# Loading the first operands of an attention into the room of finished state-space scans, and projecting its values first

## The chip, the cores and the metric

The kernel runs on one core of one Trainium2 chip. The metric is the device time of one execution in microseconds (us), lower is better; three runs of the kernel before are known, and their median stands for it.

## The reference, cut to what matters

The program computes two layers of a hybrid trunk on 640 tokens (512 latents, 128 of context) of 1024 channels, in float32. In each layer the normalised stream is projected once, and four mixers of 256 channels work on the columns; then come one output projection and a gated feed-forward part.

```
h = rmsnorm(x) * (1 + scale1) + shift1
fa, fb, fc, fd = split(h @ w_in)
oa = rwkv_mixer(fa)        # two scans
ob = retention_mixer(fb)   # two scans in chunks
oc = ssd_mixer(fc)         # state-space, two scans in chunks
od = diff_mixer(fd)        # differential attention
x = x + gate1 * (concat(oa, ob, oc, od) @ w_out)
x = x + gate2 * conv_ffn(rmsnorm(x) * (1 + scale2) + shift2)

def diff_attention(q, k, v, lam):     # per block of 128 queries and head
    s = einsum(q, k) * scale          # two maps m
    pr = softmax(s)
    return (pr[0] - lam * pr[1]) @ v
```

## The kernel before

Every product with weights is made of three passes (high times high, high times low, low times high) of float32r parts. Weights come by DMA on SP's queue through four raw buffers, ScalarE (ACT) casts the high part (line 184) and VectorE (DVE) subtracts the low part (line 185). Matmuls are recorded at line 84. A scheduler of the framework fixes the order of the instructions on each engine from the program order, priorities and its own model of times; on the chip each engine then takes its instructions in that order, and DMA issues stand in the same order on SP and ACT.

In each layer the last projections are a generator, `rest`: six tiles for the retention (`ret_proj`), then `diff_proj`, which makes the queries and keys of the attention in two tiles each (`dq`, `dk`, tile t = 0 and 1, rotated by `rope_tile` on ACT, DVE and GpSimd (POOL), split into two parts and stored to DRAM) and at its end the values `dv` (a product over all tokens by `tok_product`, stored to DRAM). Beside it run generators for the state-space scans (`ssds`), the retention (`ret`) and the modulation of later stages (`mod`). A loop takes steps from them in rounds: one step of `ssds` and of `ret`, half a step of `rest`, three quarters of one of `mod`. When `rest` has ended, `diff_open` closes the pools of the stream h (`hp`) and of the projections (`sp`), opens the pool `ds0` there and issues the twelve loads of the attention's first tile (`diff_load`, line 1189: `qs` and `ks`, six DMAs each; the values and the cached values on ACT's queue). The loads of the second tile (`ds1`) follow when the pools of retention and state-space scans are closed, and so do those of x (line 1645) and of the mixers' outputs (`out_load`: `olo` on ACT's queue, line 453, cast to `ohi` on ACT at line 199, low part on DVE at line 200).

Pools are stacks from the left and the right end of the on-chip memory. A tile that lies where an older tile lay waits for the last use of that tile.

The attention works in 20 units (t, head, tile of queries): products S on TensorE (PE), maximum on DVE (line 1216), exponential on ACT (line 1218), sum of both maps on DVE (line 1224), transposes on PE (line 1237), copies on ACT (lines 1239 and 1240), product with the values. What of the output projection doesn't need the attention (`po`, rows 2, 3, 4, 5, 0, 1 of `ohi`) runs beside it; rows 6 and 7 follow. Then `gw`, a pool of 12 raw buffers opened at the left where the attention's pools lay, takes weights of the modulation (`GF`), whose products run while the next norm is computed.

Of the kernel before, what the change touches and what calls it, by code (L numbers as in the profile page):

```python
# [23 lines left out]
# token columns: latents 0..511, a zero column, context 513..640, a zero column  # L24
# [4 lines left out]
WR = 7  # L29
PO1 = ()  # L30
DP = 9
RS = (0.5, 0.0, 0.75, 1, 1, 1, 0.5)
DU = 100
# [9 lines left out]
# columns of the per-layer parameter block  # L43
# [10 lines left out]
# columns of the constant block  # L54
# [17 lines left out]
def tile_trunk(ctx: ExitStack, tc: tile.TileContext, xT, cT, wmod, win, wv1, wv2, wout, wup, wdn, wlora, gup, pp, srw,  # L72
# [13 lines left out]
    class Pool:  # L86
        """A tile pool that can be closed out of turn; `bufs` per tag."""
# [14 lines left out]
    class Banks:  # L102
        """A half of PSUM: two pairs of banks (for the dense products) or four single banks."""
# [26 lines left out]
    def XMT(name):  # L130
        """a bank beside the dense products"""
        return sbank.tile(name)

# [23 lines left out]
    # silu(c) = u * (1 + tanh(u)), u = c / 2  # L157
# [30 lines left out]
    def w_pair(src, name):  # L188
        """the two halves (four blocks of the contraction each) of one column tile"""
        return [w_split(src[i], 512, f"{name}_{i}") for i in range(2)]  # L190
# [18 lines left out]
    def modulation(l, qs, bank=SMT, burst=False, pool=None):  # L209
        """in steps: one for each tile of weights, or (burst) for four of them"""  # L210
# [23 lines left out]
    def modulation_blocks(blocks, pool, n):  # L234
        """whole blocks, n tiles of weights loaded ahead"""
# [35 lines left out]
    def modulation_behind(l, qs, bank, pool, after):  # L271
        """loads, products and sums a step apart, each behind what runs beside it"""
# [42 lines left out]
    def spread(r, n, name, d, bank=SMT):  # L315
        """r [128 tokens, 5 * n]: rows of channels; n = 1 for all 128 channels, 2 for two heads of 64."""
# [12 lines left out]
    def x_stats(x, xp, name):  # L329
        """1/rms of x per token, spread over the partitions."""  # L330
# [21 lines left out]
    def norm(l, which, x, xp, name, before=None):  # L352
        """the stream h = rmsnorm(x) * g * (1 + scale) + shift, in two parts, zero columns between the streams"""
# [33 lines left out]
    def cm_product(parts, h, name, M=128):  # L387
        """[M channels, 2 halves of the tokens with one column of overlap on each side]"""
# [12 lines left out]
    def tok_product(l, src, n, h, name, dest):  # L401
        """token rows of h @ W: dest [128 tokens, 5, n]"""
# [19 lines left out]
    def conv(ps, out, wl, wc, wr, bias=None, M=128):  # L422
        """centred taps along the tokens, from PSUM"""
        act(v2(out), ps[:M, :, 1:322], AF.Identity, bias=0.0 if bias is None else bias, scale=wc)  # L424
        vstt(v2(out), ps[:M, :, 0:321], wl, v2(out), MULT, ADD)  # L425
        vstt(v2(out), ps[:M, :, 2:323], wr, v2(out), MULT, ADD)  # L426
# [7 lines left out]
    def head_stats(sqs, n, name, floor=None, scale=1.0 / 64, eps=EPS, bank=SMT, tg=""):  # L434
        """sqs: channel tiles [128, T] of squares -> per token and head, 1/sqrt, [128 tokens, 5 * n * len(sqs)]"""
# [8 lines left out]
    # mixer inputs and outputs wait in DRAM for their turn  # L444
# [18 lines left out]
    # ================= RWKV-7 =================  # L463
# [7 lines left out]
    def rw_proj(l, h, key, dv, out):  # L471
        """one projected tile, tokens shifted"""
# [11 lines left out]
    def rw_prep(l, t, f, dv, rw):  # L484
        """half normalised keys, and the values with tokens on partitions"""
# [10 lines left out]
    def rw_values(l, t, f, rw):  # L496
        """values with tokens on partitions: even chunks of 64 in the upper half, odd ones in the lower"""
# [18 lines left out]
    def rw_pre(l, t, d, f, wa, rw, dv, S, need):  # L516
        """up to the scores inside chunks and the right-hand sides"""
# [20 lines left out]
        # log decays, summed inside chunks of 64 with a leading (trailing) zero  # L538
# [40 lines left out]
        # scores inside chunks of 64, transposed: rows (b | k) of token j, columns (a | r) of token i  # L579
# [5 lines left out]
        for g, ms in enumerate(GRP):  # L585
# [12 lines left out]
            # the strict blocks of 32 on the diagonal  # L598
# [12 lines left out]
        def rhs():  # L611
# [4 lines left out]
            for g, ms in enumerate(GRP):  # L616
# [7 lines left out]
                # right-hand sides [a | A_ak v], tokens on partitions, two chunks a pack  # L624
# [15 lines left out]
    def rw_sub(l, t, d, rw, dv, S):  # L640
        """inverses of the 16-blocks of I - A, transposed, by substitution"""
# [19 lines left out]
        # combined to blocks of 32: X1 O X2 beside the diagonal (X2 O X1 backwards)  # L661
# [21 lines left out]
        # and to blocks of 64: what lies beside the diagonal of the inverses is X1 O X2 again  # L683
# [6 lines left out]
        for e in range(2):  # L690
            # empty in this direction
# [24 lines left out]
    def rw_solve(l, t, d, f, rw, dv, y, S):  # L716
        """solve, the chunk maps, the states from chunk to chunk, the outputs"""
# [47 lines left out]
        # states from chunk to chunk; MI = [state (key, value) ; identity]  # L765
# [37 lines left out]
    def rw_end(l, t, f, rw, dv, y):  # L803
# [5 lines left out]
        # group norm over each head  # L809
# [19 lines left out]
    # ================= projections that wait =================  # L829
    def rope_tile(ps, out, tab, sp, nm):  # L830
        """rotary pairs lie 16 partitions apart in every 32; context columns turn by 0"""
# [8 lines left out]
    def silu2(ps, o):  # L840
        """2 * silu, from PSUM"""
# [43 lines left out]
    def diff_proj(l, h, sp):  # L885
        tab = sp.tile([128, 2, 660], tag="tab", name=f"dtab{l}")
        nc.scalar.dma_start(tab[:, :, 0:T], rope[1])
        # queries and keys in two exact parts, the cache behind the keys of the tokens
        for t in range(2):
# [4 lines left out]
            for nm, src, dst in (("ck", ck[:, 0:128], [d_[:, T:T + 128] for d_ in kd]), ("dq", None, qd),  # L894
# [8 lines left out]
                for d_, part in zip(dst, (hi, lo)):  # L903
                    nc.scalar.dma_start(d_, part.bitcast(F32))
                yield
            scr[f"dq{t}{l}"], scr[f"dk{t}{l}"] = qd, kd
        tv = sp.tile([128, 5, 264], tag="tab", name=f"dv{l}")
        tok_product(l, wv2, 256, h, "dv", tv[:, :, 0:256])
        store(f"dv{l}", tv[:, :, 0:256])
# [991 lines left out]
```

## Time and profile before

| | |
|---|---|
| median of three runs | 2267.35 us |
| lowest and highest run | 2264.86 and 2267.46 us |
| span of the profiled execution, first to last instruction | 2266.5 us |
| the profiled execution's own time | not shown apart from its span; the median lies 0.85 us above the span |
| PE busy | 2136.9 us, 94% of the span |
| mean granted clock of PE | 0.963 of full speed |
| DMA | 232.26 MB, 102 GB/s over the span |

A timeline row gives start, duration, engine, line, operation, output and inputs, count and, in brackets, the idle time of the engine before it with what ended it. SPq and ACTq are DMA issues of these engines. A row of a windows answer gives, for one stretch, its length, the busy time of PE, PEld (weight loads), DVE, ACT and POOL with their instruction counts, the granted clock, the share of the 16 DMA engines that was busy, and GB/s.

### The profile page before, as it was taken

To read this page: it belongs to the slowest core of one execution; us is meant where nothing else is said; L and a number is where in the kernel's file an instruction comes from. 1 tells how busy PE (TensorE), PEld (TensorE's weight loads), DVE (VectorE), ACT (ScalarE), POOL (GpSimd) and SP (SyncE) were. 2 spreads that over 40 slices of the span, in tenths; PEclk is the share of its full clock that TensorE was granted. 3 is DMA by queue.
4 is the path that set the end of the run, shared out by engine and by line. 5 is a ranking of instruction groups with operands and counts; after the bars stand their busy time and mean duration, and the time that the engine had idled before them with its cause. 6 is when DMAs were issued, how large, how long until landed. Compare 5 with 4: busy or idle time off the path is not lost. (4 is left out here: it accounts for less than half of the span.)

```text
span 2266.5 us, 41011 instructions
## 1 busy us (share of the span) xinstructions
PE 2136.9 (94%) x16265; PEld 1936.7 (85%) x16265; DVE 1307.2 (58%) x2951; ACT 816.4 (36%) x1603; POOL 275.2 (12%) x468
## 2 busy tenths in 40 slices
PE   6999999979999999999989999999799999999997
PEld 3887887767878899999988888777678899999997
DVE  3687776547564435545457777755475654454553
ACT  4343432226343313323344334332363432232332
POOL 3111122210020000000031111222001100000002
PEclk9999999988989999999999999999799999999998
DMA  6212126575233332222332211365832222222221
GB/s 241 77 55 67 49 80 226 181 213 137 68 94 121 123 87 71 71 79 75 92 89 60 72 51 56 98 221 176 235 102 73 75 75 71 75 73 77 73 72 67
DMA packets 130943, 232.26 MB, mean 102 GB/s; under 512 B 14784, under 2 KB 34752, under 8 KB 130752
## 3 DMA queue, kind: packets, MB, share of 16 engines
q1 hardware_dynamic: 98304, 176.47, 26.4%
q10 hardware_dynamic: 32448, 53.17, 7.2%
q8 instruction: 129, 2.11, 0.4%
q14 instruction: 62, 0.51, 0.1%
HBM read 199.16 MB, written 30.42 MB: 101 GB/s over the span
## 5 line engine op out<-in xcount | busy, mean ns | idle before, releaser
L84 PE MATMUL pu<-hhi_n,wh_up 128*128 128x324 f32 x1408 | 326.9, 314 | 0.6 <-DVE gv L426 0.6
L84 PE MATMUL pu<-hlo_n,wh_up 128*128 128x324 f32 x1408 | 325.9, 313 | 0.5 <-POOL hlo_n L381 0.4
L84 PE MATMUL pu<-hhi_n,wl_up 128*128 128x324 f32 x1408 | 324.5, 312 | 0.0
L185 DVE TENSOR_TENSOR wl_up<-wr_up,wh_up 128x512 fp32r<-128x512 f32 x176 | 123.2, 706 | 236.2 <-ACT wh_up L184 232.5
L84 PEld LDWEIGHTS pu<-hhi_n,wh_up 128*128 128x128 f32 x1408 | 238.1, 190 | 16.1 <-issue 10.0
L84 PEld LDWEIGHTS pu<-hlo_n,wh_up 128*128 128x128 f32 x1408 | 239.5, 190 | 1.9 <-issue 0.8
L84 PEld LDWEIGHTS pu<-hhi_n,wl_up 128*128 128x128 f32 x1408 | 239.3, 190 | 0.0
L184 ACT CAST wh_up<-wr_up 128x512 fp32r<-128x512 f32 x176 | 108.3, 617 | 291.4 <-issue 136.5
L84 PE MATMUL pd<-gh,wh_dn 128*128 128x322 f32 x704 | 162.5, 312 | 0.0
L84 PE MATMUL pd<-gh,wl_dn 128*128 128x322 f32 x704 | 162.4, 312 | 0.0
L84 PE MATMUL pd<-gl,wh_dn 128*128 128x322 f32 x704 | 162.3, 312 | 0.0
L184 ACT CAST wh_dn<-wr_dn 128x512 fp32r<-128x512 f32 x96 | 56.0, 584 | 207.4 <-PE pd L84 148.2
L185 DVE TENSOR_TENSOR wl_dn<-wr_dn,wh_dn 128x512 fp32r<-128x512 f32 x96 | 61.9, 646 | 106.7 <-ACT wh_dn L184 105.9
L84 PEld LDWEIGHTS pd<-gh,wh_dn 128*128 128x128 f32 x704 | 119.6, 190 | 0.8 <-ACT wh_dn L184 0.8
L84 PEld LDWEIGHTS pd<-gl,wh_dn 128*128 128x128 f32 x704 | 119.3, 190 | 0.5
L84 PEld LDWEIGHTS pd<-gh,wl_dn 128*128 128x128 f32 x704 | 119.2, 190 | 0.0
L432 DVE SCALAR_TENSOR_TENSOR x<-pd,mod,x 128x322 f32<-128x322 f32 x144 | 54.5, 434 | 92.4 <-PE pd L84 92.4
L425 DVE SCALAR_TENSOR_TENSOR gv<-pu,pp,gv 128x642 f32<-128x642 f32 x88 | 78.0, 887 | 41.2 <-ACT gv L424 34.8
L84 PE MATMUL po<-ohi,wh_out 128*128 128x320 f32 (+1 forms) x256 | 79.1, 333 | 14.8 <-ACT ohi L199 14.4
L424 ACT ACTIVATE gv<-pu,pp 128x642 f32<-128x642 f32 x88 | 77.8, 884 | 39.0 <-PE pu L84 39.0
L84 PE MATMUL mps<-wr_mod,sc 128*32 128x512 f32 x384 | 77.3, 672 | 2.9 <-DMA wr_mod<-in_wmod 2.9
L426 DVE SCALAR_TENSOR_TENSOR gv<-pu,pp,gv 128x642 f32<-128x642 f32 x88 | 78.0, 886 | 3.1
(742 smaller groups left out, 4521.9 us busy)
## 6 DMA issues: line engine op xcount, KB each, us to landing
wr_mod<-in_wmod SPq DMA_DIRECT2D x192, 256.0 KB, 4.1
wr_up<-in_wup SPq DMA_DIRECT2D x176, 256.0 KB, 2.6
wr_dn<-in_wdn SPq DMA_DIRECT2D x64, 256.0 KB, 2.7
wr_dn<-in_wdn SPq DMA_DIRECT2D x32, 192.0 KB, 2.4
olo<-scr_o ACTq DMA_DIRECT2D x16, 321.0 KB, 4.6
wr_out<-in_wout SPq DMA_DIRECT2D x16, 256.0 KB, 2.6
wr_out<-in_wout SPq DMA_DIRECT2D x32, 128.0 KB, 2.1
x_in<-in_xT SPq DMA_DIRECT2D x8, 321.0 KB, 5.9
```

The source lines that it names most:

```text
L84: last_pe = nc.tensor.matmul(*a, **k).ins
L184: nc.scalar.copy(hi[:, :n], raw[:, :n])
L185: vtt(lo[:, :n], raw[:, :n], hi[:, :n].bitcast(F32), SUB)
L424: act(v2(out), ps[:M, :, 1:322], AF.Identity, bias=0.0 if bias is None else bias, scale=wc)
L425: vstt(v2(out), ps[:M, :, 0:321], wl, v2(out), MULT, ADD)
L426: vstt(v2(out), ps[:M, :, 2:323], wr, v2(out), MULT, ADD)
L432: vstt(xs, halves[j][:, o:o + n], g[:, s:s + 1], xs, MULT, ADD)
```

## The change

The values are projected first in `diff_proj`, before queries and keys. The retention's pool `mr` moves from the right end to the left one, with six raw weight buffers instead of seven (`WR`). When the state-space scans end, `diff_early` closes their pool `mp`, opens the pools of x and of the norm (`xp`, `xq`) and `ds0` at the right end in its place, and issues the first tile's loads there, provided that the first key tile is projected. `diff_open` then opens only the pool of the attention's work tiles, after the loop. `ds0` stays open until the output projection is done. The rate `RS[3]` and the count `DU`, which would start the attention inside the loop after 100 rounds, go; the loop never reached them. All other lines of the diff remove comments.

```
-WR = 7
+WR = 6
     def diff_proj(l, h, sp):
+        tv = sp.tile([128, 5, 264], tag="tab", name=f"dv{l}")
+        tok_product(l, wv2, 256, h, "dv", tv[:, :, 0:256])
+        store(f"dv{l}", tv[:, :, 0:256])
+        nc.scalar.dma_start(o_v[l], tv[:, 4, 0:256])
+        yield
         tab = sp.tile([128, 2, 660], tag="tab", name=f"dtab{l}")
...
+                if nm == "dk":
+                    scr[f"dq{t}{l}"], scr[f"dk{t}{l}"] = qd, kd
                 yield
-            scr[f"dq{t}{l}"], scr[f"dk{t}{l}"] = qd, kd
-        tv = sp.tile([128, 5, 264], tag="tab", name=f"dv{l}")
-        tok_product(l, wv2, 256, h, "dv", tv[:, :, 0:256])
-        store(f"dv{l}", tv[:, :, 0:256])
-        nc.scalar.dma_start(o_v[l], tv[:, 4, 0:256])
...
         mr = Pool(f"rr{l}", {"tokv": 1, "cs": 1, "ld": 3, "kt": 1, "vw": 2, "st": 1, "pt": 2, "qd": 2, "yy": 1, "tmp": 1,
-                             "wraw": WR}, "right")
+                             "wraw": WR})
...
+        def diff_early():
+            mp.close()
+            xps.append(Pool(f"x{l + 1}", {"x": 1}, "right"))
+            xps.append(Pool(f"xq{l + 1}", {"xs": 1, "xq": 3}, "right"))
+            ds0 = Pool(f"ds0{l}", {"v": 1, "qs": 1, "ks": 1}, "right")
+            while f"dk0{l}" not in scr:
+                pump(rest, 1)
+            ld.append(diff_load(l, 0, ds0, nc.sync))
+            xps.append(ds0)
+
         def diff_open():
             sp.close()
             hp.close()
-            ds0 = Pool(f"ds0{l}", {"v": 1, "qs": 1, "ks": 1})
-            ld.append(diff_load(l, 0, ds0, nc.sync))
             dp = Pool(f"dif{l}", {"P": 6, "at": 3, "yy": 2, "sums": 2, "eps": 2})
-            dpools.extend((dp, ds0))
+            dpools.append(dp)
...
                 if n_ in going and step(n_, g_, rate):
                     going.discard(n_)
-            if not dif and step("rest", rest, RS[6]):
-                dif = diff_open()
-                pump(dif, 1)
+                    if n_ == "ssd":
+                        diff_early()
+            step("rest", rest, RS[6])
         pump(mod)
-        if dif is None:
-            pump(rest)
-            dif = diff_open()
-            pump(dif, 1)
+        pump(rest)
         mr.close()
-        mp.close()
-        xp = Pool(f"x{l + 1}", {"x": 1}, "right")
+        dif = diff_open()
+        pump(dif, 1)
+        xp, xq, ds0 = xps
         x = xp.tile([128, KD, T], tag="x", name=f"x_{l}")
-        xq = Pool(f"xq{l + 1}", {"xs": 1, "xq": 3}, "right")
...
         pump(out_part((6, 7)))
         op.close()
+        ds0.close()
```

## Rows read from the trace of the kernel before

**Rows 1.** The page's line of the granted PE clock, 40 slices of 56.7 us

```profile
PEclk9999999988989999999999999999799999999998
```

**Rows 2.** Windows around the attention's start, first layer, then second

```profile
470.00:491.80 21.80, 21.39 (x177) 17.83 (x178) 10.04 (x22) 5.47 (x12) 1.61 (x4) 1.00 0.78 253
491.80:502.10 10.30, 5.93 (x56) 5.25 (x52) 2.89 (x9) 1.97 (x5) 2.07 (x5) 0.71 0.96 268
502.10:510.20 8.10, 1.63 (x7) 1.44 (x7) 0.19 (x2) 0.73 (x1) 1.55 (x1) 0.50 0.89 230
510.20:523.30 13.10, 11.52 (x40) 9.40 (x41) 10.58 (x17) 8.13 (x18) 0.00 (x0) 0.50 0.84 208
523.30:600.00 76.70, 70.14 (x494) 60.42 (x492) 51.12 (x120) 48.17 (x136) 3.95 (x2) 1.00 0.33 93
600.00:635.00 35.00, 34.22 (x230) 33.94 (x231) 22.27 (x52) 11.22 (x22) 7.47 (x11) 1.00 0.30 87
...
1619.00:1626.40 7.40, 1.59 (x6) 1.40 (x6) 0.00 (x0) 0.73 (x1) 1.03 (x1) 0.50 0.92 232
1626.40:1642.60 16.20, 13.25 (x46) 10.57 (x47) 11.66 (x20) 9.22 (x20) 0.00 (x0) 0.50 0.82 203
```

**Rows 3.** Timeline of PE in the first layer

```profile
499.92 1.30 PE L323 MATMUL R_ret<-cs,rsq 128*128 128x128 f32 x5 [2.91 <-DVE rsq L318]
502.09 1.62 PE L84 MATMUL S<-ks,qs 96*128 96x320 f32 x6 [0.87 <-DVE ry L926]
510.19 0.63 PE L84 MATMUL po<-ohi,wh_out 128*128 128x322 f32 x1 [6.47 <-ACT ohi L199]
```

**Rows 4.** Timeline of PE in the second layer

```profile
1618.97 1.62 PE L84 MATMUL S<-ks,qs 96*128 96x320 f32 x6 [1.45 <-DMA ks<-scr_dk0h]
1626.43 0.63 PE L84 MATMUL po<-ohi,wh_out 128*128 128x322 f32 x1 [5.84 <-ACT ohi L199]
```

**Rows 5.** Timeline of SP's DMA issues in the first layer

```profile
475.69 8.91 SPq L1645 DMA_DIRECT2D x<-in_xT  x8
...
491.84 0.38 SPq L1189 DMA_DIRECT2D qs<-scr_dq0h  x1
...
513.20 0.30 SPq L1189 DMA_DIRECT2D ks<-scr_dk0h  x1
...
548.41 5.19 SPq L177 DMA_DIRECT2D wr_mod<-in_wmod  x3
...
568.58 0.91 SPq L177 DMA_DIRECT2D wr_mod<-in_wmod  x2
```

**Rows 6.** Timeline of ACT and its DMA issues in the first layer

```profile
469.98 0.35 ACTq L450 DMA_DIRECT2D scr_o<-sy  x1
...
505.51 2.37 ACTq L453 DMA_DIRECT2D olo<-scr_o  x3
509.41 0.73 ACT L199 CAST ohi<-olo 128x642 fp32r<-128x642 f32 x1 [14.12 <-DMA olo<-scr_o]
```

**Rows 7.** Timeline of DVE in the first layer, at the attention's start

```profile
510.17 0.83 DVE L200 TENSOR_TENSOR olo<-olo,ohi 128x642 fp32r<-128x642 f32 x1 [7.91 <-ACT ohi L199]
510.91 1.55 DVE L1216 TENSOR_REDUCE mx<-S 128x1 f32<-128x640 f32 x2
```

**Rows 8.** The values' product: matmuls, min/median/max ns, first and last start

```profile
L84 PE MATMUL dv<-wh_dv,hhi_n x40: 278/283/388, 470.5 to 491.1; 128*128 128x256 f32 x40
```

**Rows 9.** Timelines of DVE and POOL during the last key tile's rotation, first layer

```profile
475.11 2.00 DVE L837 TENSOR_TENSOR rsdk<-rsdk,dtab 128x642 f32<-128x642 f32 x1
...
477.46 0.83 DVE L838 TENSOR_TENSOR st_dk<-rfdk,rsdk 128x642 f32<-128x642 f32 x1
474.89 1.54 POOL L836 TENSOR_TENSOR rfdk<-rfdk,dtab 128x642 f32<-128x642 f32 x1 [8.53 <-issue]
```

**Rows 10.** PE's idle time before modulation products: 330 to 500, 1450 to 1620 us

```profile
DMA wr_mod<-in_wmod: 5.3, 4
...
DMA wr_mod<-in_wmod: 0.7, 2
```

More of the change, by code (lines that the diff above doesn't have):

```diff
@@ L28 @@
 TAIL = (0, 0, 1, 1)
-WR = 7
+WR = 6
 PO1 = ()
 DP = 9
-RS = (0.5, 0.0, 0.75, 1, 1, 1, 0.5)
-DU = 100
+RS = (0.5, 0.0, 0.75, None, 1, 1, 0.5)
 HP = {"ssd": 300, "mod": 300}
@@ L1549, in tile_trunk @@
         ld, ys, sums, sp2 = [], {}, {}, [0, None]
-        dif, dpools = None, []
+        dpools, xps = [], []
         def bank_s(n_):
@@ L1567, in diff_open @@
             yield from diff(l, units, dp, dv, ld, ys, bank_s, sums, lambda n_: bank_s(n_)[:, 0])
-        ret, going, rounds = ret_all(), {"ssd", "ret"}, 0
+        ret, going = ret_all(), {"ssd", "ret"}
         while going:
             step("mod", mod, RS[2])
-            if dif and rounds >= DU:
-                step("dif", dif, RS[3])
-            if dif:
-                rounds += 1
             for n_, g_, rate in (("ssd", ssds, RS[4]), ("ret", ret, RS[5])):
```

## The prediction

> **What bounds the kernel now.** I read the page first for PE. It is busy over nine tenths of the span, so only stretches in which it stands still or runs at half clock can give time back. The line of the clock dips in few slices [rows 1]; the slices that begin at 453 and 1587 us lead to the starts of the attention, and there I cut windows [rows 2]. The reader is to see three stretches in each layer. While the last projections run, PE is full at full clock (21.39 of 21.80 us). From 491.8 to 502.1 us only the end of the retention is left, a chain over all engines, and the clock falls from full to its lower level, 0.50. From 502.1 to 523.3 us the clock stays there: PE is busy 1.63 + 11.52 = 13.15 of 21.2 us, which at half clock is 6.6 us of full-speed work, so 14.6 us are lost. The second layer loses 23.6 - (1.59 + 13.25) / 2 = 16.2 us from 1619.0 to 1642.6 us. From then on PE does 70.14 / 76.7 = 0.914 of what it could.
>
> Then I asked the timelines what PE waits for there. The first six products S run when the retention has let go of its PSUM bank in the first layer, and 1.45 us late, for the last `ks` that they need, in the second [rows 3, 4]. So the operands' lateness is itself worth 0 and 1.45 us. The long wait comes after S: 6.47 and 5.84 us for the first `ohi` of the output projection [rows 3, 4]. ACT casts `ohi` when `olo` has landed, at 509.41 us, and DVE's fixed order puts the low part of `olo` (510.17 us) ahead of the first maximum of S (510.91 us), though S was done at 503.71 us [rows 6, 7]. The attention so stands 7.2 us behind a load that it doesn't need. The order was fixed with S expected late: its loads can't be issued before 491.84 us, when the values' product, the last reader of h, has ended [rows 5, 8]. The DMA engines are 0.89 and 0.84 busy from 502.1 to 523.3 us [rows 2], with the rest of the first tile's twelve loads (to 513.20 us), those of the second tile and `olo` together.
>
> **The change part by part.**
>
> The values' product is moved, not changed: 40 groups of three matmuls [rows 8], its eight loads, its copies, its store. PE does it behind the retention's projections instead of behind the last key tile; both times it is filler among full rounds, and the number of steps of `rest` up to its end is 13 as before, so the last projected tile falls into the same round and PE reaches the retention's tail at the same time. Cost: nothing, hidden by PE's own queue; if the order slipped by a round, the tail would shift by at most the projection that is left over, which would cover it. What ends at 491 us is now the second key tile, whose rotation and stores follow beside the retention's tail. Its DVE multiplication took 2.00 us beside POOL's 1.54 us, the addition of the same shape 0.83 us [rows 9]. Lower bound 0 (it fits into the waits of the tail), upper bound all of its DVE time that I can see, 2.00 + 0.83 = 2.8 us per layer. Since the tail's engines mostly wait (DVE 2.89 of 10.30 us) [rows 2], I take 0.5 us per layer. The Trainium skill, SBUF — State Buffer, section "Who interferes with whom", says that a DVE instruction with two on-chip inputs contends with a POOL instruction that reads there; the trace agrees with 2.00 against 0.83 us. By that rule alone, with the tail's own POOL operations caught too, the cost would be some 1.2 us per layer instead of 0.5, and the sum 1.4 us worse.
>
> The first tile's loads can start when the last output of the state-space scans is stored (issue 469.98 us [rows 6]) instead of 491.84 us. On SP they stand among the last modulation weights and before x (eight issues in 8.91 us [rows 5]). Twelve loads of 160 to 193 KB are 2.1 MB, at the 253 GB/s of that stretch 8.4 us: done by about 490 to 495 us even behind the weights, well before 502 us. x slips by as much, to about 495 us; its first reader is the first sum behind the output products, after 510 us, so nothing waits. The values and cached values on ACT's queue also leave the tail.
>
> What this gives: S no longer waits for DMA (1.45 us, second layer), and with S expected at once the order should put its maximum before `olo`. Then from 502.1 us the attention fills PE. I take 55% of PE for the first 6 us (the chain through maximum, exponential and sum starts up; DVE and ACT work 10.58 and 8.13 of 13.1 us once it goes [rows 2]), and 95% from there, when `ohi` has come too. The clock comes back, in the trace, at 523.3 us after PE had been busy without a gap from about 516 us, and at 1642.6 us after gaps until about 1632 us; so I estimate 14 us after the start, at about 516 us. First layer, in full-speed work to 523.3 us: (0.55 * 6 + 0.95 * 8) / 2 + 0.914 * 7.2 = 12.0 against 6.6, a gain of 5.4 us. Second layer, from 1617.6 us: 5.45 + 0.914 * 11 = 15.5 against 7.4, a gain of 8.1 us. Together 13.5 us. From below the gain of this part is 0 (order unchanged, loads hidden) and from above all the loss after S, 14.6 + 16.2 = 31 us; I stand near the middle, because half clock at the restart can't be avoided: it fell in the tail, which stays.
>
> The weights' ring of the modulation shrinks from seven to six. PE waited 5.3 and 0.7 us for such weights in these stretches [rows 10]. Lower bound 0, upper bound those waits again, 6.0 us; the loads come in fours and two buffers still run ahead, so I take 0.5 us in all.
>
> `gw` now lies where the attention's work tiles lay, no longer where `ds0` lay. Its twelve loads were issued from 548.41 to 568.58 us [rows 5], when the first tile's half of the attention was through; now they wait for the last units, about 600 us. They are needed at 635 us, and the DMA engines are 0.30 busy from 600 to 635 us [rows 2]. 3.1 MB at 230 GB/s take 13.7 us. Hidden, unless SP puts them before output weights. Lower bound 0, upper bound 13.7 us less the 10 us or so by which four raw and four split buffers run ahead, 4 us per layer; I take 0.5 us per layer.
>
> `mr` on the other side, `xp` and `xq` opened earlier, `ds0` closed later: no instruction and, by the sizes, nearly the same addresses for `mr`; 0, with 2 us to either side.
>
> Sum: 13.5 - 1.0 - 0.5 - 1.0 = 11 us off the profiled span of 2266.5 us. The median is 0.85 us above that span; the same part lies around both, so I take 11 us off the median: 2256.4 us.
>
> **The rivals.**
>
> A, no change: the loads weren't what held the attention. For it: S waited 0 and 1.45 us for them [rows 3, 4]; if DVE still takes `olo` before the maximum, only 1.45 us and an earlier `olo` (at most the two value loads ahead of it on ACT, about 1.3 us a layer) come off. Against: that order is plainly one made for late loads. Gain 1.5 to 4 us: 2263 to 2266 us.
>
> B, slower: the `gw` loads. SP issues in order; if the first of them waits for the end of the attention's outputs and the output weights of rows 6 and 7 stand behind it, PE, at 34.22 of 35.00 us [rows 2], waits with nothing beside it, and the clock falls. It decides when the twelve loads stand ahead of more output weights than the buffers hold, that is, from a delay of some 10 us. Its price, with the gain lost: 4 us plus a half-clock stretch like that of the attention's start (about 4 us) per layer, 16 us against a gain of 11: 2272 us. Against: DMA is idle there, and output weights were issued early.
>
> C, slower: the ring of six doubles the waits for modulation weights (6 us, in stretches where PE has no gap now), and twelve loads on SP hold the last of them behind them, up to 8.4 us a layer; 2267 - 11 + 6 + 10 = 2272 us. Against: these loads carry a raised priority.
>
> D, more: the second key tile runs into the retention's tail and covers it too. From 491.8 to 502.1 us PE does about 5 of 10.3 us at full-speed count; covering it in both layers gives some 10 us more, 2246 us. Against: the counted rounds are the same.
>
> **How the numbers follow.** Forecast 0.48, A 0.23, B 0.12, C 0.07, D 0.10. The forecast's own range is 2250 to 2262 us, by the bounds above. Its time, 2256.4 us, is the prediction. For eight in ten the range leaves out the outer half of D and of B and C: 2246 to 2272 us. A measurement tells about 0.2%, 4.5 us, from no change: faster means below 2262.8 us, slower above 2271.9 us. Faster: 0.48 and D, 0.58. Same: A less a little that ends slower, and the milder ends of B and C, 0.25. Slower: 0.17.
>
> **What would show it.** `qs` and `ks` of the first tile issued before 485 us and landed before S; on DVE the first `mx` before the first `olo`; PE without the 6.5 us gap before `po`; clock 1.00 some 5 to 10 us sooner after S in both layers; `gw` loads at about 600 us, with PE still full to 635 us. I would be wrong if DVE's order stays, if PE shows new waits for `wr_mod` or `wh_out`, or if the last key tile holds up the retention's tail so that S itself comes later than 502 us.

## The result, and the profile after

| | before | after |
|---|---|---|
| median | 2266.83 us (8 runs, 2257.12 to 2269.36) | 2288.69 us (8 runs, 2275.90 to 2301.41) |
| span of the profiled execution | 2266.5 us | 2274.1 us |
| mean granted clock of PE in it | 0.963 | 0.970 |

The change is slower: ratio 1.0118, 95% interval 1.0093 to 1.0143, that is some 27 us (the ratio isn't the quotient of the two medians, which is 1.0096, or 21.9 us). I had predicted 2256.4 us and a range that ends at 2272. The profiled execution is the shortest of the eight after the change. Its granted clock is 0.970, that of the longest run 0.957, and the times between follow the clock: 0.013 of some 2290 us is 30 us, and the runs lie 25.5 us apart. So this trace shows only 7.6 us of the loss, and what it shows as a wait without a fall of the clock may have one in other runs.

First the page of after: the line of PE's clock, to be held against [rows 1], and the group of the modulation's products, with the same group of before under it.

```profile
PEclk9999999989999999999999999999699899999998
...
L83 PE MATMUL mps<-wr_mod,sc 128*32 128x512 f32 x384 | 92.3, 669 | 0.8 <-DMA wr_mod<-in_wmod 0.8
```

```profile
L84 PE MATMUL mps<-wr_mod,sc 128*32 128x512 f32 x384 | 77.3, 672 | 2.9 <-DMA wr_mod<-in_wmod 2.9
```

The clock is as good as before. The same 384 products, each as long as before, kept PE busy for 77.3 us on the page of before and now for 92.3 us, because fewer of them run side by side.

Then I cut both traces at the same events: the end of the gates' projection, the first S, and the first product of the feed-forward (in the second layer the last output product). Windows of before:

```profile
381.90:502.10 120.20, 110.23 (x781) 82.92 (x779) 61.46 (x140) 31.61 (x67) 25.69 (x23) 0.96 0.66 206
502.10:653.20 151.10, 130.75 (x836) 113.41 (x836) 92.56 (x206) 72.90 (x182) 15.01 (x15) 0.88 0.39 110
1499.80:1619.00 119.20, 109.65 (x781) 82.92 (x779) 62.30 (x138) 31.37 (x67) 26.30 (x24) 0.96 0.66 208
1619.00:1754.30 135.30, 120.14 (x770) 107.45 (x770) 84.23 (x185) 68.82 (x175) 12.61 (x14) 0.90 0.40 109
```

The same windows of after:

```profile
376.80:502.10 125.30, 116.44 (x781) 84.25 (x779) 56.61 (x140) 31.40 (x67) 26.71 (x23) 0.96 0.57 181
502.10:652.00 149.90, 127.02 (x835) 110.45 (x835) 94.19 (x206) 72.52 (x182) 15.03 (x15) 0.92 0.42 127
1496.40:1622.20 125.80, 116.61 (x780) 84.27 (x779) 56.49 (x138) 31.41 (x67) 26.71 (x23) 0.96 0.56 180
1622.20:1760.50 138.30, 120.28 (x770) 108.08 (x770) 85.59 (x186) 68.37 (x175) 13.20 (x14) 0.90 0.41 124
```

The loss of this trace stands ahead of the attention: +5.1 and +6.6 us between the gates' projection and the first S, at the same clock and with the same instructions. PE doesn't wait longer there: its idle time falls by 1.1 and 0.4 us, and its busy time grows by 6.2 and 7.0. The modulation's products in the first of these windows, before and after:

```profile
381.90:502.10 120.20, 23.10 (x144) 0.96 0.66 206
```
```profile
376.80:502.10 125.30, 29.69 (x144) 0.96 0.57 181
```

They grow by 6.6 us, and in the second layer by 7.6 (from 22.25 to 29.83). So what this one trace shows is the ring of six; the runs below show that most of the median's loss is another thing. In the first layer S comes at 502.1 us in both kernels all the same, because the gates' projection ends 5.1 us sooner. From S on the difference is -1.2 and +3.0 us, where I expected -5.4 and -8.1.

The waits have changed too. R_gn, R_ret and R_ssd are five transposes each, which spread the factors of a norm over the channels (of the first mixer, the retention and the state-space scans); rkt transposes the retention's keys. The timeline of PE in before, at four waits of the earlier stretch:

```profile
352.71 0.74 PE L323 MATMUL R_gn<-cs,gsr 128*128 128x128 f32 x5 [1.31 <-DVE gsr L318]
368.62 0.74 PE L917 MATMUL rkt<-cs,ldrk 128*128 128x128 f32 x5 [1.30 <-DMA ldrk<-scr_rk]
432.89 0.77 PE L323 MATMUL R_ret<-cs,rsq 128*128 128x128 f32 x5 [2.14 <-DVE rsq L318]
467.36 0.74 PE L323 MATMUL R_ssd<-cs,ssq 128*128 128x128 f32 x5 [1.36 <-DVE ssq L318]
```

and in after, with the attention's start:

```profile
344.99 0.74 PE L322 MATMUL R_gn<-cs,gsr 128*128 128x128 f32 x5 [2.07 <-DVE gsr L317]
363.17 0.74 PE L918 MATMUL rkt<-cs,ldrk 128*128 128x128 f32 x5 [2.95 <-DMA ldrk<-scr_rk]
436.82 1.23 PE L322 MATMUL R_ret<-cs,rsq 128*128 128x128 f32 x5 [3.36 <-DVE rsq L317]
474.63 1.30 PE L322 MATMUL R_ssd<-cs,ssq 128*128 128x128 f32 x5 [1.29 <-DVE ssq L317]
502.09 1.65 PE L83 MATMUL S<-ks,qs 96*128 96x320 f32 x6 [0.89 <-DVE ry L927]
508.77 1.73 PE L83 MATMUL S<-ks,qs 96*128 96x320 f32 x6 [5.04 <-ACT P L1219]
511.56 0.90 PE L83 MATMUL po<-ohi,wh_out 128*128 128x322 f32 x2 [1.06 <-ACT ohi L198]
```

Three of the four waits have grown, all of them ahead of the key tiles that I had watched. Behind the last two, five products take 1.23 and 1.30 us instead of 0.77 and 0.74: there the clock has fallen (behind R_ret it falls in before too, a little later: 0.50 from 436 to 438 us). At the attention the gap before `po` is down from 6.47 us [rows 3] to 1.06, and a new one of 5.04 us stands before the second S. SP's issues in after:

```profile
480.13 0.47 SPq L1190 DMA_DIRECT2D qs<-scr_dq0h  x1
...
508.49 0.43 SPq L1190 DMA_DIRECT2D ks<-scr_dk0h  x1
...
526.29 4.36 SPq L1648 DMA_DIRECT2D x<-in_xT  x8
...
604.05 7.06 SPq L176 DMA_DIRECT2D wr_mod<-in_wmod  x12
```

The first tile is issued from 480 us on, not from 491.84 [rows 5], but its last load still at 508 us, and x 50 us later than before. DVE and ACT in after:

```profile
503.08 1.56 DVE L1217 TENSOR_REDUCE mx<-S 128x1 f32<-128x640 f32 x2 [0.84 <-PE S L83]
...
511.59 0.83 DVE L199 TENSOR_TENSOR olo<-olo,ohi 128x642 fp32r<-128x642 f32 x1 [0.88 <-ACT ohi L198]
```

```profile
503.75 0.33 ACTq L449 DMA_DIRECT2D scr_o<-ry  x1
504.11 0.59 ACTq L452 DMA_DIRECT2D dv<-scr_dv  x1
504.75 0.68 ACTq L1194 DMA_DIRECT2D dv<-in_cvt  x1
506.95 0.83 ACTq L452 DMA_DIRECT2D olo<-scr_o  x2
507.83 0.79 ACT L1219 ACTIVATE P<-S,mx 128x640 f32<-128x640 f32 x1 [9.88 <-DMA dv<-in_cvt]
```

DVE's order has turned as predicted: the maximum (503.08 us) stands ahead of `olo` (511.59), against [rows 7]. But the exponential that needs this maximum stands on ACT behind four kinds of DMA issues, and starts at 507.83 us. The wait has moved from DVE's order to ACT's.

### The profile page after: what moved, and what is told of

Read it like the earlier page. It is cut to its first block, busy times and chain, and to the rows that moved or that the text cites. A ratio compares the mean times of both kernels' runs of the same rounds, so it can differ in the third digit from the quotient of the medians.

```text
span 2274.1 us, 41001 instructions
## 1 busy us (share of the span) xinstructions
PE 2138.9 (94%) x16265; PEld 1930.7 (85%) x16265; DVE 1305.0 (57%) x2951; ACT 815.6 (36%) x1603; POOL 276.4 (12%) x468
## 5 line engine op out<-in xcount | busy, mean ns | idle before, releaser
L83 PE MATMUL mps<-wr_mod,sc 128*32 128x512 f32 x384 | 92.3, 669 | 0.8 <-DMA wr_mod<-in_wmod 0.8
L83 PE MATMUL po<-ohi,wh_out 128*128 128x322 f32 (+1 forms) x256 | 77.7, 326 | 4.9 <-ACT ohi L198 4.3
```

The lines of the kernel that those rows point to most:

```text
L83: last_pe = nc.tensor.matmul(*a, **k).ins
```

## The experiments

Each ratio is to the kernel before, run beside it on the same chip.

| run | median us | ratio, 95% interval |
|---|---|---|
| after | 2288.69 | 1.0118 (1.0093 to 1.0143) |
| b_w6: before, ring of six | 2268.30 | 1.0029 (1.0007 to 1.0051) |
| b_w8: before, ring of eight | 2261.05 | 0.9995 (0.9975 to 1.0016) |
| a_w7s: after, ring of seven | 2287.44 | 1.0101 (1.0075 to 1.0127) |
| a_w7v: after, ring of seven, first values late | 2292.79 | 1.0146 (1.0114 to 1.0177) |
| a_w6v: after, ring of six, first values late | 2297.56 | 1.0163 (1.0132 to 1.0195) |
| b_vf: before, values first | 2298.08 | 1.0146 (1.0127 to 1.0165) |
| b_v1: before, values second | 2263.48 | 1.0010 (0.9994 to 1.0027) |
| b_vm: before, values between the tiles | 2268.12 | 1.0025 (1.0010 to 1.0041) |
| a_vm: after, values between the tiles | 2278.58 | 1.0070 (1.0049 to 1.0091) |
| a_vl7: after, values last, ring of seven | 2268.71 | 1.0025 (1.0007 to 1.0043) |
| a_vl7_sp: that, store from SP | 2274.51 | 1.0053 (1.0034 to 1.0072) |
| a_vl7_sp_ol3: that, output operands later | 2269.68 | 1.0021 (1.0007 to 1.0035) |
| b_sp: before, store from SP | 2269.57 | 1.0026 (1.0012 to 1.0039) |
| a_xe: after, x early | 2297.37 | 1.0140 (1.0119 to 1.0161) |
| a_eo: after, olo from POOL | 2315.39 | 1.0215 (1.0181 to 1.0250) |
| a_hp: after, retention raised | 2306.34 | 1.0195 (1.0161 to 1.0230) |
| b_vf_hp: values first, retention raised | 2319.93 | 1.0251 (1.0225 to 1.0277) |
| a_vl7_hp: a_vl7, retention raised | 2319.88 | 1.0251 (1.0221 to 1.0281) |

**The ring.** Two kernels differ from before by one number. a_w7v differs from after by it and by the first tile's values (3 KB for each partition), which had to move to make room, its twin a_w6v by the values alone, and a_w7s makes room by sharing the norms' buffers.

```diff
-WR = 7
+WR = 6            # b_w6; 8 in b_w8; from 6 to 7 in a_w7v and a_w7s
```
```diff
-            ds0 = Pool(f"ds0{l}", {"v": 1, "qs": 1, "ks": 1}, "right")
+            ds0 = Pool(f"ds0{l}", {"qs": 1, "ks": 1}, "right")
...
-        ds1 = Pool(f"ds1{l}", {"v": 1, "qs": 1, "ks": 1}, "right")
+        ds1 = Pool(f"ds1{l}", {"v": 2, "qs": 1, "ks": 1}, "right")
```
```diff
-            xps.append(Pool(f"xq{l + 1}", {"xs": 1, "xq": 3}, "right"))
+            xps.append(Pool(f"xq{l + 1}", {"xq": 3}, "right"))
```

b_w6: 

> The kernel before with a ring of six modulation weights in place of seven, nothing else. Theory ring: with six buffers only two of the next step's four weights can land while a step's four are still held, so the four products of a step, which stand in four different column groups of PE, are no longer issued side by side but as x4, x2, x2; the group mps<-wr_mod,sc grows from 77.3 us to about 92 us, as in the kernel after, and the time by 8 to 15 us, to 2275 to 2282 us. Theory queues (the loss sits in the first tile's loads and in what stands behind them on SP and ACT): no such loads are moved here, so 2267 us, within 3 us, even if the products lie apart.

b_w8: 

> The kernel before with a ring of eight, two whole steps. Theory ring: all four products of every step stand side by side, mps<-wr_mod,sc falls below 77 us, to about 70 us, and the time by 3 to 7 us, to 2260 to 2264 us. Theory queues: 2267 us, within 3 us.

a_w7v: 

> The kernel after with a ring of seven again; for its room the first tile's values (not its queries and keys) are loaded with the second tile's operands. Theory ring: mps<-wr_mod,sc is back at about 77 us and the time 10 to 15 us below the twin with six, about 2265 to 2275 us. Theory queues: as the twin with six, within 3 us.

a_w6v: 

> The twin: the kernel after with its ring of six, and the first tile's values loaded with the second tile's operands. Both theories: as the kernel after, 2276 to 2292 us, with mps<-wr_mod,sc at about 92 us; if it is faster than that, the values' place on ACT's queue was part of the loss.

a_w7s: 

> The kernel after with a ring of seven; the room comes from letting the sum of squares of the norms share the three buffers of the squares. Theory ring: mps<-wr_mod,sc falls from 92.3 to about 80 us, the stretch before the first S by 5 us a layer, the time by 6 to 12 us against the kernel after, to about 2272 to 2280 us. Theory loads: no more than 3 us below the kernel after.

The mechanism is there. The timeline of PE in after shows two steps of the modulation, eight passes each for four tiles of weights:

```profile
407.00 1.07 PE L83 MATMUL mps<-wr_mod,sc 128*32 128x512 f32 x8
...
409.85 1.05 PE L83 MATMUL mps<-wr_mod,sc 128*32 128x512 f32 x4
...
411.71 1.05 PE L83 MATMUL mps<-wr_mod,sc 128*32 128x512 f32 x2
...
414.18 1.05 PE L83 MATMUL mps<-wr_mod,sc 128*32 128x512 f32 x2
```

Eight passes in four column groups together take 1.07 us, and two alone take 1.05. The second step's four tiles come in pieces here, four passes, two and two, and cost three times 1.05. The Trainium skill, TensorEngine Tiling (Array Packing), section "Key Properties", says that different tiles of the array can work in parallel; the trace agrees, and by that rule a ring that doesn't hold the next step whole loses this. The group measured 82.6 us in b_w6, 75.1 in b_w8, 81.4 and 82.9 in a_w7s and a_w7v, 91.0 in a_w6v. But the time follows only in part: b_w6 lost 0.29%, 6.5 us, with the expected 8 us as its least; b_w8 gained nothing that can be measured; a seventh buffer gave the changed kernel 0.17%, with overlapping intervals. The ring is a part of the loss, and by the medians a small one, although the group of products shrinks by 10.9 us from after to a_w7s. The mean clock of a_w7s's four runs is 0.955 to 0.964, that of after's eight 0.957 to 0.970, so a lower clock may take back what the ring gives; that isn't shown. Late first values cost about 0.45% (a_w7v against a_w7s).

**The place of the values.** One kernel has only this part of the change, two others put the values elsewhere, and a_vm does so in the changed kernel (the latter three load the rotation table once more).

```diff
     def diff_proj(l, h, sp):
+        tv = sp.tile([128, 5, 264], tag="tab", name=f"dv{l}")
+        tok_product(l, wv2, 256, h, "dv", tv[:, :, 0:256])
...
+        yield             # b_vf: here; b_v1: ahead of the first keys; b_vm, a_vm: ahead of tile 1
         tab = sp.tile([128, 2, 660], tag="tab", name=f"dtab{l}")
```

b_vf: 

> The kernel before with one thing of the change alone: the product of the values stands first among the attention's projections; ring of seven, loads, x and pools as before. Theory order: the retention's work then meets the turned tiles (queries and keys, with their rotations) instead of the values, and the stretch from the gates' projection to the first S grows by 5 us a layer; time 2270 to 2278 us. Theory loads (the order of the projections costs nothing; the loss comes from the early operands and from what they push back): 2262 to 2268 us, as before.

b_vm: 

> The kernel before with the product of the values between the two tiles of queries and keys (the rotation table is loaded once more for it, on ACT's queue). Theory first tile (half or more of the loss of values first comes where the first retention tile's norm meets a rotation on POOL and where ldrk is late): half of the 34 us or less is left, 2270 to 2282 us. Theory tail (it comes from the last key tile at the end, whose cast stands ahead of the retention's square on ACT): most of it is left, 2285 to 2300 us.

b_v1: 

> The kernel before with the product of the values second, behind the first tile of queries (the rotation table is loaded once more). Theory gates (the loss of values first comes from what stands directly behind the gates' projection): the first tile of queries stands there again, the waits for R_gn, ldrk and R_ssd are as in the kernel before, and at most 10 us are lost, 2264 to 2274 us. Theory amount (each projection that comes behind the values, not ahead of them, adds to the loss): between the values in the middle and the values first, 2278 to 2292 us.

a_vm: 

> The kernel after (ring of six, early loads with the values among them) with the product of the values between the two tiles of queries and keys. Theory order (the loss of the change is the place of the values, the rest adds the ring's 6 us and nothing else): 2266 to 2276 us, 15 us below the kernel after. Theory loads (the early loads cost where the values don't stand first): 2280 us or more.

This is the cause of most of the loss. Values first alone costs 34 us, more than the whole change; values second cost 2 us within the error. One pair of changed kernels differs by nothing else: a_w7v and a_vl7 (below) both have the ring of seven and late first values, and with the values last instead of first the ratio falls from 1.0146 to 1.0025. The timeline of PE in b_vf:

```profile
349.95 0.81 PE L323 MATMUL R_gn<-cs,gsr 128*128 128x128 f32 x5 [2.08 <-DVE gsr L318]
...
371.32 1.30 PE L918 MATMUL rkt<-cs,ldrk 128*128 128x128 f32 x5 [3.10 <-DMA ldrk<-scr_rk]
...
442.97 1.30 PE L323 MATMUL R_ret<-cs,rsq 128*128 128x128 f32 x5 [3.31 <-DVE rsq L318]
...
481.31 1.30 PE L323 MATMUL R_ssd<-cs,ssq 128*128 128x128 f32 x5 [1.29 <-DVE ssq L318]
```

These are the waits of after to a tenth or two: 2.1, 3.1, 3.3 and 1.3 us. Windows of 5 us in b_vf show what R_gn's and R_ret's waits cost beyond their own length:

```profile
345.00:350.00 5.00, 2.92 (x22) 2.68 (x22) 2.31 (x5) 0.62 (x1) 4.06 (x2) 1.00 0.20 52
350.00:355.00 5.00, 5.00 (x16) 3.17 (x17) 2.54 (x5) 0.52 (x2) 0.14 (x2) 0.55 0.17 66
...
440.00:445.00 5.00, 2.03 (x8) 1.40 (x9) 2.67 (x5) 0.81 (x2) 2.30 (x2) 0.76 0.20 72
445.00:450.00 5.00, 5.00 (x19) 4.33 (x20) 0.84 (x2) 0.45 (x2) 1.54 (x1) 0.55 0.47 167
```

PE stands still for some 2 or 3 us, and then works the next five at 0.55. I summed busy time times (1 - clock) over such windows from 20 us ahead of the gates' projection to the end of the last projection, for both layers: 5.0 us in before, 3.3 in b_w6, 7.8 in b_v1, 9.0 in b_vm, 21.6 in b_vf (and 14.5 in b_w8, 11.5 of it in one stretch of the second layer, so a single execution can have it without a cause in the kernel). In the changed kernel it is 5.4 in the shortest run, whose clock held behind the first two waits, and 15.4 in a_w6v, 22.5 in a_w7v, 14.5 in a_w7s, 12.5 in a_xe. Over the whole span the same sum is 57.3 us in before and 72.1 in b_vf, and PE's idle time grows from 129.6 to 144.8 us. So of the 29.8 us by which these two executions differ, about half is the lower clock and half is waiting. The clock is no chance of one execution: its mean is 0.954 to 0.957 in all four runs of b_vf, and 0.963 to 0.970 in the seven of before beside them. By place, 10.5 us lie at the end: from the last projection to S, b_vf needs 16.5 and 16.1 us in the two layers against 10.7 and 11.4, in the first because ACT's order there puts the last key tile's cast ahead of the retention's square (505.03 and 505.67 us, the input of the square being ready at 501.7). The same waits of PE in b_v1, summed by what they wait for, first layer from 340 to 500 us:

```profile
PE R_ret L323 <- DVE rsq L318: 4.7, 2, 2.9
...
PE rkt L921 <- DMA ldrk<-scr_rk: 1.5, 1, 1.5
PE R_gn L323 <- DVE gsr L318: 1.3, 1, 1.3
```

R_gn and rkt are back to 1.3 and 1.5 us, and the clock falls only once in that stretch (465 to 475 us, 0.66). The tail can't be the main cause: b_v1 and b_vm too end with the last key tile, their tails are 5.1 and 6.1 us longer than in before, and they lose 2 and 6 us in all. I had thought of the meeting of the first retention tile's norm with a rotation on POOL; in b_vm it is still there (R_ret waits 3.43 us), and the time isn't. What counts is which projection the program puts directly behind the gates'. The waits that grow don't stand behind it themselves: on PE, R_gn comes ahead of the gates' projection (360.8 to 386.3 us in b_vf), rkt inside it, and the values only from 391.8 us on. So the place of the values changes the planner's order of what comes ahead of them. In the second layer only R_gn's wait goes with the loss (1.3 us in before, b_v1 and b_vm, 2.1 in b_vf); rkt waits 2.1, 3.1, 1.2 and 2.7 us there. a_vm takes 0.48% of the 1.18 off the changed kernel, 11 us, less than the 15 expected (its early loads also wait until the values are projected), and its time lies between those of the two theories.

**The retention raised in the planner's order.** I tried to cure the values-first order by priority, in three kernels:

```diff
-HP = {"ssd": 300, "mod": 300}
+HP = {"ssd": 300, "mod": 300, "ret": 300}
```

a_hp: 

> The kernel after with a raised priority for the retention's instructions in the planner (300, as the scans and the modulation have), so that in the fixed orders of ACT and POOL they stand ahead of the casts and rotations of the key tiles; no work is added or left out. Theory order: the loss of values first lies in those two queues, so the retention's norm no longer waits behind rotations (R_ret's wait back to 2 us, no fall of the clock behind it) and the retention is done under the cover of the last projections: 15 to 30 us below the kernel after, 2258 to 2273 us. Theory PE (the values' product was the better filler for PE by its own length): 2280 to 2290 us.

b_vf_hp: 

> The kernel before with the product of the values first, as in the run of that alone, and the same raised priority for the retention. Theory order: the cost of values first alone (34 us) falls by at least half, 2262 to 2280 us. Theory PE: it stays, 2290 us or more. The operands are loaded late here, so the first S may wait for them after the last key tile.

a_vl7_hp: 

> Early loads, values last, ring of seven and the raised priority together. Theory order: the retention is done earlier and the last projections cover its tail; 5 us below the same without the priority, 2245 to 2253 us. Theory PE: no difference to the same without the priority, within 3 us.

All three are slower, by 17 to 51 us than without it. The norm waits less (R_ret at most 1.9 us), but in two of them the retention now asks for its operands before they are back: rkt waits 5.9 us in a_hp and 7.7 us in b_vf_hp for ldrk (0.8 us in a_vl7_hp, where S waits 10.4 us for exponentials instead), and in these two the attention starts only after the delayed projections (S at 528.7 and 541.8 us). My expectation failed, and the experiment doesn't separate the two queues from PE's work.

**The early loads by themselves.** The changed kernel with the values last and the ring of seven; then with the retention's last store taken off ACT, and with the loads of olo behind the third unit; and the store alone.

```diff
-        yield             # values first
...
+        tok_product(l, wv2, 256, h, "dv", tv[:, :, 0:256])     # a_vl7: after the last key tile
...
-        store(f"o{l}_{k}", o)
+        store(f"o{l}_{k}", o, nc.sync if k == 3 else nc.scalar)   # _sp
...
-OL = (1, 3)
+OL = (3, 2)                                                     # _ol3
```

a_vl7: 

> The kernel after with the order of the projections of before (the product of the values last) and a ring of seven; the first tile's queries and keys are still loaded early, its values with the second tile's. Theory order (the values-first order costs the 30 us that it cost alone, the early loads by themselves gain): 10 us below the kernel before, 2250 to 2258 us; the stretch from the gates' projection to the first S is 119 to 122 us as before, ldrk and R_ret wait no longer than before. Theory loads (the early loads themselves cost): 2272 us or more.

a_vl7_sp: 

> Early loads of queries and keys, values last, ring of seven, and the retention's last output stored from SP's queue instead of ACT's. Theory ACT (the early loads gain nothing because the first exponentials stand on ACT behind that store and behind casts that wait for its reload): the first P runs by 493 us while the retention ends, five P stand ahead of the first cast, PE waits less than 4 us for S in the 20 us behind it, and the time is 8 to 14 us below the kernel before, 2248 to 2255 us. Theory filler (what sets the time is when olo is back, since only the output products can fill PE): within 4 us of the run without this edit, 2264 to 2272 us.

a_vl7_sp_ol3: 

> The same, and the loads of the output operands placed behind the third unit of the attention instead of the first. Theory ACT: as the run before or 2 to 4 us better, since no exponential stands behind a cast that waits. Theory filler: 3 to 8 us worse than the run before, since the output products start later.

b_sp: 

> The kernel before with the retention's last output stored from SP, nothing else; the operands are loaded late as before. Theory ACT: the gain of the early loads needs both, so this alone is within 6 us of the kernel before, on either side. Theory filler: slower by 5 us or more, since the planner lets olo slip behind the first units.

The early loads of queries and keys gain nothing (a_vl7 and the two made from it load the first tile's values late). In a_vl7 all twelve are issued between 471.3 and 482.8 us, S begins at 490.2 us, 12 us sooner than before, and the feed-forward at 651.4 instead of 653.2, from a gates' projection that ended 2.8 us sooner: no gain. Only the first half of S is that early. PE in a_vl7:

```profile
490.22 0.56 PE L83 MATMUL S<-ks,qs 96*128 96x320 f32 x3
...
496.89 0.96 PE L83 MATMUL S<-ks,qs 96*128 96x320 f32 x3 [0.62 <-DVE ry L926]
```

and ACT:

```profile
498.80 0.38 ACTq L449 DMA_DIRECT2D scr_o<-ry  x1
499.23 0.79 ACT L1221 ACTIVATE P<-S,mx 128x640 f32<-128x640 f32 x1 [8.50 <-POOL ry L929]
...
508.20 0.73 ACT L198 CAST ohi<-olo 128x642 fp32r<-128x642 f32 x1 [7.31 <-DMA olo<-scr_o]
```

The first exponential waits for the second half of S, whose maximum is done at 498.7 us, and stands behind the store of the retention's last output; the second unit's stands behind the cast that waits for the reload of that store: the attention still can't start before the retention has ended. With the store on SP the first one comes no sooner. ACT in a_vl7_sp:

```profile
500.66 0.80 ACT L1221 ACTIVATE P<-S,mx 128x640 f32<-128x640 f32 x1 [8.26 <-DVE mx L1219]
...
515.30 0.73 ACT L198 CAST ohi<-olo 128x642 fp32r<-128x642 f32 x1 [7.47 <-DMA olo<-scr_o]
```

Its maximum waits for an S that found a bank of PSUM only when the retention had let it go (498.81 us, behind ry). Five exponentials do stand ahead of the first cast then, as I expected, but the operands of `po` come 7 us later, and units of the attention alone fill 1.9 to 3.7 of every 5 us of PE. The clock is full again at 528 us, in a_vl7 at 521, in before at 523.3 [rows 2]. The time that theory ACT forecast didn't come, but neither did its first exponential by 493 us: ACT's order alone doesn't hold the attention. The filler explains the sign of a_vl7_sp, which is slower than a_vl7 by more than its 4 us (the intervals overlap), but not a_vl7_sp_ol3, whose still later operands were expected to cost 3 to 8 us and which is 0.32% faster instead. b_sp lies within 6 us of before, as both theories allow. That half of the first S can be had 12 us sooner, and the rest 5 us, without a gain is shown; what sets the last 6 us either way is open.

**What the early loads push back.** x ahead of the operands, and olo on POOL's queue:

```diff
+            for k in range(KD):
+                EX.dma_start(xt_[0][:, k], xsrc[:, k])      # a_xe: in diff_early, before the operands
...
-    EO, EX, ED = nc.scalar, nc.sync, nc.sync
+    EO, EX, ED = nc.gpsimd, nc.sync, nc.sync                # a_eo
```

a_xe: 

> The kernel after with the eight loads of x issued ahead of the first tile's operands, in the place where the room becomes free, as the kernel before issues them. Theory loads: x is there before the first output product is done, the first addition to x comes at about 543 us instead of 555 us, the output products fill PE beside the attention again, and S to the first pu falls by 2 to 4 us a layer: 4 to 8 us below the kernel after. Theory ring or order: the first operands come later by eight loads, S is unchanged or later; within 3 us of the kernel after, or slower.

a_eo: 

> The kernel after with the loads of olo issued by POOL instead of ACT, so that the first exponential isn't queued behind loads that wait for the retention's store. Theory loads: the first P starts by 505 us instead of 507.83 us, the second S waits under 2 us instead of 5.0 us, the clock comes back sooner: 3 to 6 us below the kernel after. Theory ring or order: within 3 us of the kernel after.

Both are slower. In a_xe SP issues the first operand at 502.78 us behind x, and S begins at 526.7 us. In a_eo POOL issues olo only at 523.36 us, as its wait for the DMA of `qs` stands in front, and PE waits 12.3 us in two waits for `ohi`. The late x of the changed kernel wasn't worth curing in this way.

## Why the prediction was wrong

- **The values' product, "Cost: nothing, hidden by PE's own queue".** This step failed. The instructions do cost the same and are hidden; their place costs 34 us alone (b_vf), and at any later place 2 to 6 us (b_v1, b_vm). I looked for the cost where the values had stood, at the tail, and not around the place they went to. In b_vf R_gn and rkt, ahead of the gates' projection and inside it, wait 0.8 and 1.8 us longer in the first layer, the clock is 0.50 to 0.66 behind them, and the tail is 10.5 us longer in the two layers. Why the planner's order lengthens just these waits I can't show; the runs with a raised priority didn't tell.
- **"A gain of 5.4 us" and "8.1 us. Together 13.5 us".** This failed too: a_vl7 gives +0.25% where it should give -0.6%. S did start sooner there and DVE's order did turn, but I followed the chain to DVE only. In the changed kernel itself the loads, "done by about 490 to 495 us", were issued up to 508.49 us. ACT's order and a bank of PSUM hold it to the end of the retention, and the output operands come no sooner. With values first, the early loads are worth 0.45% (b_vf to a_w7s), some 10 us, of a loss that the order itself had made, and only with the first values among them: a_w7v, which loads these late, has the ratio of b_vf, 1.0146.
- **The ring, 0.5 us with bounds of 0 and 6.0.** 6.5 us in b_w6. I priced waits for weights (they fell, from 2.9 to 0.8 us on the page) and not the four products that no longer run side by side. The 5.3 and 0.7 us of [rows 10] hold waits of the weight loads (PEld) too; PE itself waited 2.1 and 0.2 us.
- **The second key tile beside the tail, "0.5 us per layer".** From the last projection to S it is 12.5 and 13.0 us in after, against 10.7 and 11.4: some 1.7 us a layer, inside the bound of 2.8.
- **x, "about 495 us".** It came at 526 us, because it stands behind both tiles' operands.
- **`gw`, "hidden".** Right: issued from 604.05 us, and PE is busy 35.00 of the 35.00 us to 635. Rival B is out.
- **The rivals.** C has the right sign, and its ring costs what I gave it, by another mechanism. None of the four is the one that happened.

The parts don't add up: 1.46, 0.29 and 0.25% are 2.0, and the change has 1.18. The early loads, with the values among them, shorten the tail (12.5 us from the last projection to S in after, 14.7 with late values in a_w7v, 16.5 in b_vf) and so take part of the first back; the rest of the difference is open. No version here beats the kernel before.

## What to carry to other kernels

A product that is moved without a change in its work is to be priced where it arrives, and ahead of that place too, since a planner orders anew: list PE's waits there, and ask for each whether it grows. Before an operand is loaded earlier, follow the first result through every engine's fixed order up to the instruction that fills PE; if one of them stands behind another chain, the load is early for nothing. A ring that feeds products in groups wants whole groups.

## What I had not expected of the hardware

The clock's answer to a gap differs: behind R_ssd's wait of 1.36 us it stayed full in before, and behind 1.29 us it was 0.52 in the next 5 us in b_vf. The changed kernel, with several gaps of 1.3 to 3.4 us, spread over 25.5 us in eight runs; but b_vf, with the same gaps, had a mean clock of 0.954 to 0.957 in its four runs and spread over 3.9 us, so the gaps alone don't set the spread. And one DVE operation takes over three times as long beside POOL. It in before:

```profile
L956 DVE TENSOR_SCALAR vw<-tokv,csr x4: 404/408/420, 364.1 to 365.9; 128x320 f32<-128x320 f32 x4
```

and in b_vf, where `tokv` lands 3 us later and POOL's `qd` (1264 ns each) runs at the same time:

```profile
L957 DVE TENSOR_SCALAR vw<-tokv,csr x4: 421/1396/1427, 367.1 to 370.9; 128x320 f32<-128x320 f32 x4
```

The Trainium skill, SBUF — State Buffer, section "Who interferes with whom", has this operation among those that can, under conditions on their operands, take the port pair shared with POOL and then wait for a whole POOL instruction; 408 against 1396 ns agrees. In after it is 1395 ns as well, in b_v1 414.
